# A k tile of the normed input 64 bytes off, and its two high products first in each chunk

## The chip, the cores and the metric

The kernel runs on one core of a Trainium2 chip. Its time is the device time of one execution in microseconds; the figure is the median of several executions. Of the engines, TensorE (PE in the profile; PEld is its loading of weights) multiplies matrices, VectorE (DVE) and ScalarE (ACT) work elementwise, GpSimd (POOL) does the rest, and SyncE (SP) issues the transfers of the weights.

## The reference, cut to what matters

Two layers work on 256 tokens of width 1024 in float32. Each layer norms its input, multiplies it with one wide matrix, feeds the parts to a sparse attention and to a state space scan, merges both with gates, projects, and adds a gated feed-forward block with a short convolution.

```python
for l in range(DEPTH):
    h = rms_norm(x, norm_mix_w[l])
    x = x + hybrid_mixer(h, w_in[l], ...)      # h @ w_in: q, k, v, index, z, xbc, dt, gates
    h = rms_norm(x, norm_ffn_w[l])
    x = x + conv_glu_ffn(h, ffn_w_up[l], ...)  # h @ w_up: 1024 x 5632; then w_down: 2816 x 1024
return rms_norm(x, norm_final_w)
```

In `conv_glu_ffn` the product `h @ w_up` goes through a causal convolution of width 3, one half through silu, and the product of both halves meets `w_down`.

## The kernel before, in words

A product in float32 is made of three products in a faster format: input and weights are each split into a high part and a low remainder, and high·high, high·low and low·high are added up in one accumulator. Weights come in chunks of 128 x 1024 numbers. SP loads a chunk into one of five `raw` buffers; ACT copies its high part (`whi`, line 199) and DVE subtracts it (`wlo`, line 200), into one of three pairs of buffers; a few chunks a layer are split early into tiles borrowed from activations (`ex`, `ez`, `es` and others in the trace). `take` (line 188) hands the next pair to the products and keeps loads and splits going. It then lets the side steps of the norm, the attention and the scan issue their instructions behind the last low product (`st["mm"]`), so that their products of other kinds come between those of the chunks.

`n_outer` (lines 390 to 397) computes 128 output columns for all 256 tokens: eight k tiles, each with a weight tile of 128 x 128, loaded into the array, and an input tile of 128 x 256 that moves through it. `feed_high` (line 367) issues whi·hi (line 370) and whi·lo (line 371) for each k, then `feed_low` (line 373) issues the eight wlo·hi (line 376): 24 products a chunk. `k_outer` does the same for four output tiles at once, over k, in a part of the projections.

The moving inputs are: the normed input `hxh`/`hxl`, [128, 8, 256] each, made by `Normed.scaled` (lines 341 to 349) and used by 92 `n_outer` chunks a layer (56 in the mix stage: convolution inputs, gates, z; 36 in the up projection); `uh`/`ul`, the input before the norm's factor; `aH`/`aL` (attention), `bH`/`bL` (scan), `mH`/`mL` (merged) and `fH`/`fL` (feed-forward), all split the same way. The last is cut over six pairs of tiles, the third and later ones of which lie in other tags than the first two. `row_of` (line 298) multiplies a matrix of ones with a diagonal `dg`, which is one of the foreign products in the stream.

A tile lies at one start address within each of the 128 partitions; pools and tags are laid out one behind the other, so a tag that grows moves all that lie after it. `mH`, the norm's `xw` and one early chunk share the tag of `hxh`. The small tile `dec` of the scan lies ahead of it.

Of the kernel before, what the change touches and what calls it, by code (L numbers as in the profile page):

```python
# [9 lines left out]
F32 = mybir.dt.float32  # L10
F32R = mybir.dt.float32r
# [7 lines left out]
P = 128  # L19
L = 2  # L20
T = 256
D = 1024
KD = D // P
# [8 lines left out]
TOPK = 64  # L32

RAW_BUFS = 5
SPLIT_BUFS = 3

FIRST_PAIRS = 4
# [25 lines left out]
def hybrid_kernel(ctx: ExitStack, tc: tile.TileContext, a: dict, out: bass.AP):  # L63
    nc = tc.nc

    const = ctx.enter_context(tc.tile_pool(name="const", bufs=1))
    wraw = ctx.enter_context(tc.tile_pool(name="wraw", bufs=RAW_BUFS))
    wsp = ctx.enter_context(tc.tile_pool(name="wsp", bufs=SPLIT_BUFS))
    act = ctx.enter_context(tc.tile_pool(name="act", bufs=1))
# [4 lines left out]
    def pst(tag, shape, bufs):  # L74
        t = psum.tile([P, 512], F32, name=tag, tag=tag, bufs=bufs)
        n = int(np.prod(shape[1:]))
        v = t[:shape[0], :n]
        if len(shape) == 3:
            v = v.rearrange("p (a b) -> p a b", a=shape[1])
        return v  # L80
# [88 lines left out]
    def load_some():  # L169
        while st["dma"] < len(order) and st["dma"] < st["prep"] + RAW_BUFS:  # L170
            i = order[st["dma"]]
            src, b, c = chunks[i]
            r = wraw.tile([P, 8 * 128], F32, name="raw", tag="raw")
            nc.sync.dma_start(r[:, :b * c].rearrange("p (b c) -> p b c", b=b), src)
            raws[i] = r[:, :b * c]
            st["dma"] += 1

    def split_tiles(j):
        if j in early:
            t0, t1 = early[j]  # L180
            if t0 == t1:
                t = act.tile([P, 2, 8 * 128], F32R, name=f"e{t0}", tag=t0)
                return [t[:, 0], t[:, 1]]
            return [(tmp if t in ("Xt", "pT") else act).tile([P, 8 * 128], F32R, name=f"e{t}", tag=t, bufs=1)
                    for t in (t0, t1)]
        return [wsp.tile([P, 8 * 128], F32R, name=t, tag=t) for t in ("whi", "wlo")]

    def take():
        i = st["cur"]
        with tc.high_priority():  # L190
            load_some()
            while st["prep"] < len(order):
                j = order[st["prep"]]
                if j not in early and sum(k not in early for k in splits) == SPLIT_BUFS:
                    break
                src, b, c = chunks[j]
                hi, lo = (t[:, :b * c] for t in split_tiles(j))
                r = raws.pop(j)
                nc.scalar.copy(out=hi, in_=r)  # L199
                nc.vector.tensor_sub(lo, r, hi.bitcast(F32))  # L200
                splits[j] = [t.rearrange("p (b c) -> p b c", b=b) for t in (hi, lo)]
                st["prep"] += 1
                load_some()
        st["cur"] += 1
        if st["mm"] is not None:
            side_steps()
        return splits.pop(i)
# [95 lines left out]
    class Normed:  # L303


        def __init__(self, nw, split=True):
            self.nw = nw
            self.acc = tmp.tile([P, T], F32, name="ssq", tag="ssq", bufs=3)
            if split:
                self.h = [act.tile([P, 4, T], F32R, name=f"uh{i}", tag=t) for i, t in enumerate(("Bm", "Cm"))]  # L310
                self.l = [act.tile([P, 4, T], F32R, name=f"ul{i}", tag=t) for i, t in enumerate(("lg0", "lg1"))]
            else:
                self.xw = act.tile([P, KD, T], F32, name="xw", tag="hxh")
            self.split = split

        def hi(self, k):
            return self.h[k // 4][:, k % 4, :]

        def lo(self, k):
            return self.l[k // 4][:, k % 4, :]  # L320
# [18 lines left out]
                nc.scalar.activation(self.xw[:, k, :], x, AF.Copy, scale=self.nw[:, k:k + 1])  # L339

        def scaled(self):
            h = act.tile([P, KD, T], F32R, name="hxh", tag="hxh")
            l = act.tile([P, KD, T], F32R, name="hxl", tag="hxl")
            for k in range(KD):
                t = tmp.tile([P, T], F32, name="ht", tag="ct", bufs=3)
                nc.vector.scalar_tensor_tensor(t, xT[:, k, :], self.nw[:, k:k + 1], self.row, op0=OP.mult, op1=OP.mult)
                nc.scalar.copy(out=h[:, k, :], in_=t)
                nc.vector.tensor_sub(l[:, k, :], t, h[:, k, :].bitcast(F32))
            return (lambda k: h[:, k, :]), (lambda k: l[:, k, :])

        def factor(self):
            ps = pst("sb", [P, 2], 2)
# [11 lines left out]
    def acc_tile():  # L364
        return pst("acc", [P, T], 4)

    def feed_high(ps, wh, hi, lo, ks, first):

        for j, k in enumerate(ks):
            nc.tensor.matmul(ps, wh[:, j, :], hi(k), start=first and j == 0, stop=False)  # L370
            nc.tensor.matmul(ps, wh[:, j, :], lo(k), start=False, stop=False)  # L371

    def feed_low(ps, wl, hi, ks, last):

        for j, k in enumerate(ks):
            st["mm"] = nc.tensor.matmul(ps, wl[:, j, :], hi(k), start=False, stop=last and j == len(ks) - 1)  # L376
# [13 lines left out]
    def n_outer(parts):  # L390

        ps = acc_tile()
        for i, (hi, lo, ks) in enumerate(parts):
            wh, wl = take()
            feed_high(ps, wh, hi, lo, ks, i == 0)
            feed_low(ps, wl, hi, ks, i == len(parts) - 1)
        return ps


# [5 lines left out]
    for l in range(L):  # L405
# [90 lines left out]
        dA = act.tile([P, 2, 32], F32, name="dA", tag="dA")  # L496
        Pc = act.tile([P, 2, 32], F32, name="Pc", tag="Pc")
        nP = act.tile([P, 2, 32], F32, name="nP", tag="nP")
        dec = act.tile([P, 32], F32, name="dec", tag="dec")

        prd = dram.tile([32, 2, P], F32, name=f"prd{l}")

# [36 lines left out]
        for c in range(5):  # L539
            n = 308 if c < 2 else 512  # L540
            pss = [pst("acc", [P, n], 4) for _ in range(2)]
            for j in range(4):
                wh, wl = take()
                for kk in range(2):
                    k = 2 * j + kk
# [28 lines left out]
        hi, lo = nrm.scaled()  # L574
# [69 lines left out]
        def conv_tile(i, dst):  # L644
            ps = n_outer([(hi, lo, range(KD))])
            v = tmp.tile([P, T], F32, name="cv", tag="cv", bufs=3)
            nc.scalar.activation(v, ps, AF.Identity, scale=cw(l, 3, i), bias=cb(l, i))  # L647
            for j in range(1, 4):
                nc.vector.scalar_tensor_tensor(v[:, j:], ps[:, :T - j], cw(l, 3 - j, i), v[:, j:],  # L649
                                               op0=OP.mult, op1=OP.add)  # L650
            th = tmp.tile([P, T], F32, name="ct", tag="ct", bufs=3)
            nc.scalar.activation(th, v, AF.Tanh)
            nc.vector.scalar_tensor_tensor(dst, th, 1.0, v, op0=OP.add, op1=OP.mult)

        def gate(t):
            ps = n_outer([(hi, lo, range(KD))])
            nc.scalar.activation(t, ps, AF.Tanh, scale=0.5)  # L657
            return t
# [101 lines left out]
        def gate_and_project(n):  # L760
            finish("attn")
            th = gate(tmp.tile([P, T], F32, name="gv", tag="cv", bufs=3))
            ps = n_outer([(lambda k: aH[k // 4][:, k % 4, :], lambda k: aL[k // 4][:, k % 4, :], range(8))])
            nc.vector.scalar_tensor_tensor(mg[n], th, 1.0, ps, op0=OP.add, op1=OP.mult)
# [24 lines left out]
        for g in range(4):  # L789
            finish("scan", 3 - g)  # L790
            y = xs[g]
            for i in range(4):
                ps = n_outer([(hi, lo, range(KD))])
# [14 lines left out]
            gate_and_project(n)  # L808


        mH = act.tile([P, KD, T], F32R, name="mH", tag="hxh")
        mL = act.tile([P, KD, T], F32R, name="mL", tag="hxl")
        bh = lambda k: bH[k // 4][:, k % 4, :]
        bl = lambda k: bL[k // 4][:, k % 4, :]
# [58 lines left out]
        hi, lo = nrm.scaled()  # L873
# [16 lines left out]
        for n in range(4, 8):  # L890
            ps = n_outer([(fh, fl, range(0, 8)), (fh, fl, range(8, 16)), (fh, fl, range(16, 22))])
# [6 lines left out]
    for c in range(2):  # L898
        for h in range(2):
            ps = pst("acc", [P, 512], 4)  # L900
# [93 lines left out]
```

## Time and profile before

| what | before |
|---|---|
| median of 3 runs | 1090.22 us (1088.49 to 1091.21) |
| the profiled execution | 1091.08 us, span 1089.1 us |
| TensorE busy | 1064.4 us, 98% |
| DVE, ACT, POOL busy | 81%, 64%, 6% |
| products of 128 x 256 with split weights | 7,416 |
| HBM | 175 GB/s over the span |

The span is the time from the first to the last recorded instruction. The profile models the end of a product, so its length (0.28 us) says little: products overlap, and what counts is the distance from one start to the next. In a timeline, neighbours of one line are drawn together with their count; the start of the next row then tells how long they took.

### The profile page before, as it was taken

How to read it: one execution, taken by the hardware profiler on the slowest of the kernel's cores; microseconds unless marked ns; L12 is line 12 of the kernel's file. 1: busy time of each engine (PE TensorE's matmuls, PEld its weight loads, DVE VectorE, ACT ScalarE, POOL GpSimd, SP SyncE). 2: the span in 40 equal slices, each digit the busy share in tenths (PEclk: the TensorE clock that was granted, in tenths of full speed). 3: DMA queues.
4: the chain of work that ended last, by engine and by line, in shares of the span. 5: the costliest groups of instructions: out<-in, count | busy, mean ns of one | idle time of the engine just before them, and what ended most of it. 6: DMA issues, size and time to landing. Idle time of an engine off the chain costs nothing.

```text
span 1089.1 us, 22471 instructions
## 1 busy us (share of the span) xinstructions
PE 1064.4 (98%) x8704; PEld 1026.2 (94%) x8704; DVE 877.9 (81%) x1755; ACT 696.2 (64%) x1285; POOL 66.5 (6%) x74
## 2 busy tenths in 40 slices
PE   6999999999999999998999999999999999999997
PEld 5789989999999999998997999999999999999997
DVE  6898988879877899885668999887887878888643
ACT  5658878647555576665555699865665556666552
POOL 3000000022000200000100000000310020000010
PEclk9999999999999999999999999999999999999999
DMA  7546444555677346666645654555567761666661
GB/s 266 183 148 213 151 147 156 161 169 175 194 233 251 117 122 195 194 199 211 183 134 176 224 155 139 164 172 155 175 190 216 246 216 45 182 187 191 180 182 48
DMA packets 52841, 191.82 MB, mean 176 GB/s; under 512 B 5952, under 2 KB 6240, under 8 KB 51712
## 3 DMA queue, kind: packets, MB, share of 16 engines
q1 hardware_dynamic: 50832, 180.31, 53.8%
q0 software_dynamic: 1472, 9.17, 2.3%
q8 instruction: 68, 1.11, 0.4%
q10 hardware_dynamic: 432, 0.92, 0.2%
q14 instruction: 37, 0.30, 0.1%
HBM read 189.26 MB, written 1.11 MB: 175 GB/s over the span
## 4 chain that ended last, share of the span: by engine, by line
PE 85%; DMA 5%; ACT 4%; DVE 3%; issue 2%; DVEq 0%; ACTq 0%; POOLq 0%
PE acc L370 23%; PE acc L371 23%; PE acc L376 23%; PE acc L550 3%; PE acc L551 2%; PE acc L549 2%; DMA bc<-prd 2%; DMA raw<-in_wu_dram 2%; PE sb L705 1%; DVE wlo L200 1%; ACT whi L199 1%; PE sa L461 1%; DVE ul L327 1%; PE sa L589 1%; PE sa L614 1%
## 5 line engine op out<-in xcount | busy, mean ns | idle before, releaser
L199 ACT CAST whi<-raw 128x1024 fp32r<-128x1024 f32 (+2 forms) x320 | 331.9, 1040 | 225.1 <-PE acc L371 168.7
L200 DVE TENSOR_TENSOR wlo<-raw,whi 128x1024 fp32r<-128x1024 f32 (+2 forms) x320 | 387.0, 1212 | 107.5 <-ACT whi L199 103.1
L370 PE MATMUL acc<-hxh,whi 128*128 128x256 f32 x1456 | 353.3, 282 | 1.0 <-ACT ths L657 0.9
L371 PE MATMUL acc<-hxl,whi 128*128 128x256 f32 x1456 | 351.2, 281 | 0.0
L370 PEld LDWEIGHTS acc<-hxh,whi 128*128 128x128 f32 x1456 | 274.6, 189 | 2.7 <-issue 1.1
L371 PEld LDWEIGHTS acc<-hxl,whi 128*128 128x128 f32 x1456 | 274.7, 189 | 2.2 <-issue 1.9
L376 PE MATMUL acc<-hxh,wlo 128*128 128x256 f32 x1456 | 202.2, 280 | 0.0
L376 PEld LDWEIGHTS acc<-hxh,wlo 128*128 128x128 f32 x1456 | 183.0, 189 | 0.7 <-issue 0.7
L370 PE MATMUL acc<-fH,whi 128*128 128x256 f32 x352 | 84.6, 280 | 2.8 <-DVE xT L833 2.8
L371 PE MATMUL acc<-fL,whi 128*128 128x256 f32 x352 | 84.4, 280 | 0.0
L649 DVE SCALAR_TENSOR_TENSOR cv<-acc,half,cv 128x255 f32<-128x255 f32 (+2 forms) x144 | 67.1, 474 | 3.9 <-ACT cv L647 3.4
L370 PEld LDWEIGHTS acc<-fH,whi 128*128 128x128 f32 x352 | 66.6, 190 | 3.1 <-issue 3.0
L851 DVE SCALAR_TENSOR_TENSOR cv<-acc,small,cv 128x255 f32<-128x255 f32 (+1 forms) x144 | 68.4, 477 | 1.3
L371 PEld LDWEIGHTS acc<-fL,whi 128*128 128x128 f32 x352 | 66.6, 189 | 0.0
L370 PE MATMUL acc<-bH,whi 128*128 128x256 f32 x256 | 62.4, 280 | 0.1
L371 PE MATMUL acc<-bL,whi 128*128 128x256 f32 x256 | 62.3, 282 | 0.0
L337 POOL TENSOR_TENSOR ssq<-ssq,sq 128x256 f32<-128x256 f32 x30 | 27.1, 904 | 516.8 <-ACT sq L333 516.2
L549 PE MATMUL acc<-whi,uh 128*128 128x512 f32 (+1 forms) x112 | 42.0, 392 | 9.2 <-ACT whi L199 9.2
L376 PE MATMUL acc<-fH,wlo 128*128 128x256 f32 x352 | 50.1, 281 | 0.0
L370 PEld LDWEIGHTS acc<-bH,whi 128*128 128x128 f32 x256 | 48.1, 188 | 0.4 <-issue 0.4
L371 PEld LDWEIGHTS acc<-bL,whi 128*128 128x128 f32 x256 | 48.2, 188 | 0.0
L695 ACT ACTIVATE bc<-bc,nP 128x128 f32<-128x128 f32 x128 | 39.9, 390 | 11.6 <-DMA bc<-prd 11.5
(281 smaller groups left out, 1873.0 us busy)
## 6 DMA issues: line engine op xcount, KB each, us to landing
raw<-in_wu_dram SPq DMA_DIRECT2D x88, 512.0 KB, 3.6
raw<-in_wx_dram SPq DMA_DIRECT2D x48, 512.0 KB, 3.6
raw<-in_wd_dram SPq DMA_DIRECT2D x38, 512.0 KB, 3.7
raw<-in_wz_dram SPq DMA_DIRECT2D x32, 512.0 KB, 3.6
raw<-in_wp_dram SPq DMA_DIRECT2D x32, 512.0 KB, 4.4
raw<-in_wq_dram SPq DMA_DIRECT2D x24, 512.0 KB, 4.5
raw<-in_wgs_dram SPq DMA_DIRECT2D x16, 512.0 KB, 3.6
bc<-prd POOLq DMA_DIRECT2D x8, 1024.0 KB, 7.3
```

The lines of the kernel that those rows point to most:

```text
L199: nc.scalar.copy(out=hi, in_=r)
L200: nc.vector.tensor_sub(lo, r, hi.bitcast(F32))
L337: nc.gpsimd.tensor_add(self.acc, self.acc, sq)
L370: nc.tensor.matmul(ps, wh[:, j, :], hi(k), start=first and j == 0, stop=False)
L371: nc.tensor.matmul(ps, wh[:, j, :], lo(k), start=False, stop=False)
L376: st["mm"] = nc.tensor.matmul(ps, wl[:, j, :], hi(k), start=False, stop=last and j == len(ks) - 1)
L549: nc.tensor.matmul(pss[t], nrm.hi(k)[:, s], wh[:, kk, :], start=f, stop=False)
L550: nc.tensor.matmul(pss[t], nrm.hi(k)[:, s], wl[:, kk, :], start=False, stop=False)
L551: st["mm"] = nc.tensor.matmul(pss[t], nrm.lo(k)[:, s], wh[:, kk, :], start=False, stop=e)
L649: nc.vector.scalar_tensor_tensor(v[:, j:], ps[:, :T - j], cw(l, 3 - j, i), v[:, j:], op0=OP.mult, op1=OP.add)
L695: nc.scalar.activation(E[:, h, :], E[:, h, :], AF.Relu, bias=nP[:, c, 8 * g + h:8 * g + h + 1])
L851: nc.vector.scalar_tensor_tensor(v[:, j:], uu[:, :T - j], fw(l, 2 - j, i), v[:, j:], op0=OP.mult, op1=OP.add)
```

## The change

The tile `hxh` gets 16 more numbers (64 B). Its k tile 0 stays at the start, the other seven lie 64 B further on. Other users of the tag leave the first 64 B out. `dec` is made 64 B longer, so that `hxh` itself starts 64 B later. In every part of an `n_outer` chunk the order of the first three products is high weights with high input, low weights with high input, high weights with low input, all for the first k tile; the pairs of the others follow, then the low weights of the others. The order applies to every user of `n_outer`, the 64 B to the normed input alone.

```diff
--- before.py
+++ after.py
@@ -32,6 +32,8 @@
 TOPK = 64
 
 RAW_BUFS = 5
+
+SHIFT = 16
 SPLIT_BUFS = 3
 
 FIRST_PAIRS = 4
@@ -175,9 +177,15 @@
             raws[i] = r[:, :b * c]
             st["dma"] += 1
 
+    def shifted(name, dtype):
+        return act.tile([P, SHIFT + KD * T], dtype, name=name, tag="hxh")[:, SHIFT:].rearrange("p (k t) -> p k t", k=KD)
+
     def split_tiles(j):
         if j in early:
             t0, t1 = early[j]
+            if t0 == "hxh":
+                t = shifted("ehxh", F32R).rearrange("p (a k) t -> p a (k t)", a=2)
+                return [t[:, 0], t[:, 1]]
             if t0 == t1:
                 t = act.tile([P, 2, 8 * 128], F32R, name=f"e{t0}", tag=t0)
                 return [t[:, 0], t[:, 1]]
@@ -310,7 +318,7 @@
                 self.h = [act.tile([P, 4, T], F32R, name=f"uh{i}", tag=t) for i, t in enumerate(("Bm", "Cm"))]
                 self.l = [act.tile([P, 4, T], F32R, name=f"ul{i}", tag=t) for i, t in enumerate(("lg0", "lg1"))]
             else:
-                self.xw = act.tile([P, KD, T], F32, name="xw", tag="hxh")
+                self.xw = shifted("xw", F32)
             self.split = split
 
         def hi(self, k):
@@ -339,14 +347,15 @@
                 nc.scalar.activation(self.xw[:, k, :], x, AF.Copy, scale=self.nw[:, k:k + 1])
 
         def scaled(self):
-            h = act.tile([P, KD, T], F32R, name="hxh", tag="hxh")
+            h = act.tile([P, SHIFT + KD * T], F32R, name="hxh", tag="hxh")
+            hs = [h[:, 0:T]] + [h[:, SHIFT + k * T:SHIFT + (k + 1) * T] for k in range(1, KD)]
             l = act.tile([P, KD, T], F32R, name="hxl", tag="hxl")
             for k in range(KD):
                 t = tmp.tile([P, T], F32, name="ht", tag="ct", bufs=3)
                 nc.vector.scalar_tensor_tensor(t, xT[:, k, :], self.nw[:, k:k + 1], self.row, op0=OP.mult, op1=OP.mult)
-                nc.scalar.copy(out=h[:, k, :], in_=t)
-                nc.vector.tensor_sub(l[:, k, :], t, h[:, k, :].bitcast(F32))
-            return (lambda k: h[:, k, :]), (lambda k: l[:, k, :])
+                nc.scalar.copy(out=hs[k], in_=t)
+                nc.vector.tensor_sub(l[:, k, :], t, hs[k].bitcast(F32))
+            return (lambda k: hs[k]), (lambda k: l[:, k, :])
 
         def factor(self):
             ps = pst("sb", [P, 2], 2)
@@ -392,8 +401,12 @@
         ps = acc_tile()
         for i, (hi, lo, ks) in enumerate(parts):
             wh, wl = take()
-            feed_high(ps, wh, hi, lo, ks, i == 0)
-            feed_low(ps, wl, hi, ks, i == len(parts) - 1)
+            k = ks[0]
+            nc.tensor.matmul(ps, wh[:, 0, :], hi(k), start=i == 0, stop=False)
+            nc.tensor.matmul(ps, wl[:, 0, :], hi(k), start=False, stop=False)
+            nc.tensor.matmul(ps, wh[:, 0, :], lo(k), start=False, stop=False)
+            feed_high(ps, wh[:, 1:], hi, lo, ks[1:], False)
+            feed_low(ps, wl[:, 1:], hi, ks[1:], i == len(parts) - 1)
         return ps
 
 
@@ -496,7 +509,7 @@
         dA = act.tile([P, 2, 32], F32, name="dA", tag="dA")
         Pc = act.tile([P, 2, 32], F32, name="Pc", tag="Pc")
         nP = act.tile([P, 2, 32], F32, name="nP", tag="nP")
-        dec = act.tile([P, 32], F32, name="dec", tag="dec")
+        dec = act.tile([P, 32 + SHIFT], F32, name="dec", tag="dec")[:, :32]
 
         prd = dram.tile([32, 2, P], F32, name=f"prd{l}")
 
@@ -808,7 +821,7 @@
             gate_and_project(n)
 
 
-        mH = act.tile([P, KD, T], F32R, name="mH", tag="hxh")
+        mH = shifted("mH", F32R)
         mL = act.tile([P, KD, T], F32R, name="mL", tag="hxl")
         bh = lambda k: bH[k // 4][:, k % 4, :]
         bl = lambda k: bL[k // 4][:, k % 4, :]
```

## Rows read from the trace of the kernel before

**Rows 1.** The page's first part: busy us, share of the span, instructions
```profile
PE 1064.4 (98%) x8704; PEld 1026.2 (94%) x8704; DVE 877.9 (81%) x1755; ACT 696.2 (64%) x1285; POOL 66.5 (6%) x74
```

**Rows 2.** The page's fourth part: the chain that ended last, by engine
```profile
PE 85%; DMA 5%; ACT 4%; DVE 3%; issue 2%; DVEq 0%; ACTq 0%; POOLq 0%
```

**Rows 3.** The page's fifth part: first group of weight products
```profile
L370 PE MATMUL acc<-hxh,whi 128*128 128x256 f32 x1456 | 353.3, 282 | 1.0 <-ACT ths L657 0.9
```

**Rows 4.** Windows: stretch, length, busy us (instructions) by engine, clock, DMA
```profile
385.97:483.90 97.93, 97.93 (x866) 97.93 (x865) 89.78 (x153) 67.89 (x113) 0.00 (x0) 1.00 0.62 185
483.91:549.09 65.18, 62.36 (x529) 62.19 (x528) 37.99 (x47) 31.50 (x46) 4.93 (x6) 0.97 0.66 197
915.56:1017.32 101.76, 101.76 (x866) 101.76 (x865) 89.56 (x153) 68.43 (x113) 0.00 (x0) 1.00 0.60 177
1017.32:1078.83 61.51, 61.51 (x530) 61.41 (x528) 28.54 (x32) 26.81 (x38) 5.07 (x6) 1.00 0.46 137
89.75:92.63 2.88, 2.88 (x26) 2.88 (x25) 0.81 (x1) 2.88 (x8) 0.00 (x0) 1.00 0.62 248
70.95:289.52 218.57, 217.26 (x1843) 208.01 (x1842) 190.11 (x406) 158.86 (x334) 17.43 (x16) 1.00 0.55 170
```

**Rows 5.** Timeline of TensorE: start, length, line, count; an early tile
```profile
91.56 0.28 PE L371 MATMUL acc<-hxl,ex 128*128 128x256 f32 x1
91.68 1.12 PE L376 MATMUL acc<-hxh,ex 128*128 128x256 f32 x8
92.63 0.28 PE L370 MATMUL acc<-hxh,whi 128*128 128x256 f32 x1
92.75 0.28 PE L371 MATMUL acc<-hxl,whi 128*128 128x256 f32 x1
```

**Rows 6.** Timeline of TensorE: `hxh` ends, `fH` begins, layer 0
```profile
483.23 0.84 PE L376 MATMUL acc<-hxh,wlo 128*128 128x256 f32 x6
483.91 0.28 PE L370 MATMUL acc<-fH,whi 128*128 128x256 f32 x1
484.03 0.28 PE L371 MATMUL acc<-fL,whi 128*128 128x256 f32 x1
```

**Rows 7.** Timeline of TensorE: from `fH`'s second tile to its third
```profile
494.27 1.10 PE L376 MATMUL acc<-fH,wlo 128*128 128x256 f32 x8
495.22 0.28 PE L370 MATMUL acc<-fH,whi 128*128 128x256 f32 x1
495.33 0.28 PE L371 MATMUL acc<-fL,whi 128*128 128x256 f32 x1
```

**Rows 8.** Timeline of TensorE: end of a `bH`/`bL` chunk
```profile
302.70 0.29 PE L371 MATMUL acc<-bL,whi 128*128 128x256 f32 x1
302.83 0.28 PE L370 MATMUL acc<-bH,whi 128*128 128x256 f32 x1
303.06 1.11 PE L376 MATMUL acc<-bH,wlo 128*128 128x256 f32 x8
304.01 0.28 PE L370 MATMUL acc<-bH,whi 128*128 128x256 f32 x1
```

**Rows 9.** Timeline of TensorE: the same with a row product
```profile
826.88 0.28 PE L298 MATMUL sb<-dg,ones 128*128 128x256 f32 x1
827.00 0.28 PE L371 MATMUL acc<-bL,whi 128*128 128x256 f32 x1
827.11 1.07 PE L376 MATMUL acc<-bH,wlo 128*128 128x256 f32 x8
828.02 0.28 PE L370 MATMUL acc<-bH,whi 128*128 128x256 f32 x1
```

**Rows 10.** Timelines of DVE and TensorE: a `wlo` tile, its first use
```profile
357.37 1.22 DVE L200 TENSOR_TENSOR wlo<-raw,whi 128x1024 fp32r<-128x1024 f32 x1
...
360.20 1.11 PE L376 MATMUL acc<-mH,wlo 128*128 128x256 f32 x8
```

**Rows 11.** Waits: engine, line, releaser: us in total, times, longest
```profile
ACT whi L199 <- PE acc L371: 168.7, 143, 5.4
```

## The prediction

> **What bounds the kernel now.** The page's busy shares come first: TensorE is busy for 98% of the span, at full granted clock [rows 1]. The chain that ended last runs through TensorE for 85% of the span, most of it the lines of the weight products [rows 2]. So the kernel ends when 7,416 products of 256 columns have been streamed, and the question is how far apart they start. `n_outer` with the normed input issues 184 chunks of 24 of them, 4,416 in all.
>
> Then the table of windows. The same 864 products of the up projection take 97.93 us in layer 0 and 101.76 us in layer 1 [rows 4], nothing else between them (the counts of 866 hold the two products that reach in from before): 113.3 and 117.8 ns from start to start. I call the two cadences F and S. Both hold for 36 chunks without a break, with the same code and data sizes, so a state lasts until something disturbs it. A third, E, is in the timeline where the weights lie in an early-split tile: 120 ns from start to start [rows 5], 24 products in 2.88 us [rows 4]. What sets E apart is addresses. In the compiled kernel before, `whi` and `wlo` start 64 B past a multiple of 512 in their partition, `hxh` and `hxl` at a multiple; the early tile `ex` starts at a multiple too, as `hxh` does. In E moving tile and weight tile have one position modulo 256 B. Otherwise the moving tile lies 64 B below the weights.
>
> All products at S instead of F would cost 4.44 ns each. Counting starts in the timeline, the excess over 113.3 ns (gaps of 130 ns and more left out) is 0.0 and 3.84 us in the two up projections, 3.94 and 3.96 us in the two mix stages (465 and 445 of 1,344 starts at F, 835 and 849 at S, layer 0's window holds 1,843 products in all [rows 4], layer 1's as many); 11.7 us in all. `fH` has 0.78 and 1.61 us (528 products in each of its windows [rows 4]), `aH` 0.67 us. That is what a change of this kind can give back.
>
> What moves the state? A jump of the moving address, or a foreign product. From `hxh` to `fH`, layer 0 goes from F to S within one product [rows 6]; at the fourth chunk boundary after, S goes to F [rows 7]. In `bH`/`bL` chunks every second product has its moving tile at the weights' position modulo 256 B (`bL`, as E) and the rest 64 B above it (`bH`). The eight `wlo` products that end such a chunk, all `bH`, then run at S: 0.95 us from first to next chunk [rows 8]. Of 32 such tails, 29 are S. Three are F, and two of these are the two where the row product `dg` (96 B off its weights) comes right ahead of the last `bL` product, so that two odd products follow each other: 0.91 us [rows 9].
>
> **The change, part by part.**
> *Addresses.* `dec` grows by 64 B and `hxh` starts after it: k tile 0 then lies 64 B past a multiple of 512, exactly where `whi` and `wlo` lie, which is the relation of E. The other k tiles, `hxl`, `mH`, `aH` and `fH` from its third tile on move by 128 B, to 64 B above the weights, the relation that `bH` and the first two tiles of `fH` have already. `bH`, `bL` and `uh` keep their places.
> *Order.* Each part of an `n_outer` chunk starts whi·hi0, wlo·hi0, whi·lo0; the rest is as before. Instructions, DMAs and bytes are the same in number, so nothing is added on ACT, DVE, POOL or SP. With `hxh`, each of 182 chunks (184 less the two with early tiles) starts with two products in E's relation.
> *The kick's own price.* Two products at 120 instead of 113.3 ns [rows 5, 4]: 13.3 ns from F, 4.4 ns from S. The exit was free behind E (92.63 to 92.75 us is 117 to 118 ns [rows 5]). I take 13.3 ns x 182 = 2.4 us; the ends are 0.8 us (all from S) and 5.5 us (30 ns: the longest interval behind a `bL` product is 0.13 us [rows 8], two of these are some 30 ns over two at F).
> *The state behind it.* This decides. 13.3 ns is three times 4.44, just the sum by which three S products fall behind F, so two E products put the stream off by one whole S period: from F the phase would be F's again. From S the nearest rows are the two pairs of odd products, and both ended in F, at the relation that `hxh` will have [rows 9]. I take F behind each kick. Against it stand the 29 tails behind a single one [rows 8], and both exits from E after 24 products, to S [rows 5].
> *What is left of S.* Foreign products fall into 21 and 27 of the 56 mix chunks per layer; behind the last one in a chunk 290 and 313 products remain. At S to the chunk's end they cost 603 x 4.44 ns = 2.7 us, at half that 1.3; I take 2.0 us.
> *`fH` and `aH`.* All of `fH` past its first two tiles now has the relation of these, so the jump between them [rows 7] goes. F lasts then if it enters in F. The bounds are -2.4 us (all F) and +2.2 us (all S: 4.6 for 2.4); I take -1.0. `aH`: -0.7 to +1.0, taken as 0.
> *`wlo` earlier.* It is wanted 15 products, 1.7 us, sooner. Between the end of `wlo`'s subtraction on DVE and its first product the median is 5.8 us, and the shortest in `n_outer` is in the `mH` chunk: DVE ends at 358.59 us, the first `wlo` product starts at 360.20 [rows 10]. With `wlo` wanted at 358.4 that chunk waits 0.2 us; the same in layer 1: +0.4 us. Behind a waiting product stands all of TensorE. If the cover were gone everywhere each chunk would wait for DVE; with 5.8 us I put that at nothing.
> *`whi` one product longer.* ACT waits 168.7 us in all for `whi` buffers, 143 times [rows 11]; their release comes 0.12 us later each time. TensorE's first products with `hxh` sat idle for 1.0 us in all, behind ACT's `ths` and not behind `whi` [rows 3], so this costs nothing; were ACT the bound, 0.12 us a chunk.
>
> Sum for the likeliest case: `hxh` 2.4 + 2.0 - 11.7 = -7.3, `fH` -1.0, `wlo` +0.4: -7.9 us on the profiled 1091.1, so 1083.2. The median of the runs shown is 0.9 below that execution, which makes 1082.3; I say 1082.5.
>
> [...]
>
> **The rivals.**
> *A, the kick locks the slow state.* Every `hxh` chunk then runs at S. For it: 29 of 32 tails behind an odd product at the very relation that `hxh` gets [rows 8], both exits from E [rows 5], and F to S at the jump to `fH`'s first tiles, which have that relation too [rows 6]. Against it: the two pairs [rows 9]. Price: 4,416 x 4.44 ns less the starts behind gaps, 19.2 us, for 11.7 now: +7.5; kicks from S +0.8; `aH` up to +1.0, `fH` up to +2.2; +0.4 for `wlo`. +8.7 to +11.9, 1099 to 1102. It beats the gain as soon as over 60% of the products stay at S, which is today's share (11.7 of 19.2).
> *C, no lasting lock.* The state behind a kick depends on the phase in which it comes, and each chunk draws anew; or it hangs on something else than the address. Half at S: 9.6 us + kicks of 8.9 ns x 182 = 1.6, 11.2 for 11.7 now; with `fH` and `aH` to either side 1088 to 1093, 1090 in the middle. For it: the foreign products of the mix stage change the state in about half the cases and not in the others. [...]
> *D, `wlo` comes late.* If DVE's lead shrinks because TensorE runs faster, waits of the size of that in [rows 10] spread. Tens of them cost 4 us; DVE is busy for 81% [rows 1], against.
>
> **How the numbers follow.** Likeliest, F behind each kick: 0.50, own range 1079 (kick cheap, all of `fH` F) to 1087 (kick 5.5, 2.7 left, `fH` no better). A: 0.26, C: 0.22, D: 0.02. The range 1079 to 1099 leaves out half of A, D, and a little below. 0.3% is 3.3 us, about what a measurement of this kernel can tell from no change. Faster by more: 0.47 + 0.03 of C. Within: 0.03 of the likeliest, 0.15 of C. Slower: A, D and the rest of C, 0.32.
>
> **What would show it.** After the change, the windows of the two up projections should both last some 98.4 us (864 x 113.3 ns + 36 kicks of 13.3 ns); the first two intervals of each chunk 240 ns together; in the mix stages each chunk's first products at F whatever came before. If each is some 102 us, A holds; if the layers or the chunks differ, C. I am wrong if F is entered by only some kicks, if the kick costs more than 30 ns, or if products wait at the second slot of a chunk.

## The result, and the profile after

The changed kernel takes 1097.11 us in the median of 5 runs (1095.77 to 1097.99), the kernel before 1088.49 in as many. The ratio is 1.0084, with a 95% interval of 1.0060 to 1.0108: slower, by rival A's mechanism.

First the changed kernel's page, the first and fourth part and two groups of the fifth (line, tiles, count, busy us and mean ns of one, idle time before).

```profile
PE 1071.8 (98%) x8704; PEld 1033.4 (94%) x8704; DVE 877.7 (80%) x1755; ACT 695.6 (64%) x1285; POOL 65.7 (6%) x74
...
PE 91%; DMA 3%; DVE 3%; issue 1%; ACT 1%; DVEq 0%; ACTq 0%; POOLq 0%
...
L379 PE MATMUL acc<-hxh,whi 128*128 128x256 f32 x1274 | 311.2, 280 | 0.0
...
L405 PE MATMUL acc<-hxh,whi 128*128 128x256 f32 x182 | 53.4, 294 | 0.1
```

TensorE is as full as before [rows 1] and its part of the chain has grown from 85% to 91% [rows 2]: the products themselves got longer in sum, 1071.8 us busy for 1064.4, with the same 8,704 of them. Next the table of windows (stretch, length, busy us and count by engine, clock, DMA): layer 0's mix stage, its up projection, the down projection, and layer 1's up projection.

```profile
70.85:289.29 218.44, 218.34 (x1843) 209.65 (x1842) 189.72 (x406) 159.08 (x334) 16.92 (x16) 1.00 0.54 170
386.41:488.18 101.77, 101.77 (x867) 101.77 (x865) 89.50 (x154) 67.69 (x114) 0.00 (x0) 1.00 0.60 178
488.18:550.39 62.21, 62.21 (x530) 62.13 (x528) 38.40 (x47) 31.86 (x46) 5.12 (x6) 1.00 0.67 207
919.64:1021.41 101.77, 101.77 (x866) 101.77 (x865) 89.18 (x153) 66.92 (x113) 0.00 (x0) 1.00 0.59 177
```

Against [rows 4]: the up projection of layer 0 has gone from 97.93 to 101.77 us, layer 1's stays at 101.77, both now 117.8 ns a product. Counting from start to start, the weight products' excess over 113.3 ns (gaps of 130 ns and more apart) rises by 9.3 us: up projections +3.8, mix stages from 3.94 and 3.96 to 5.43 and 5.62 (+3.2), `fH` from 0.78 and 1.61 to 2.34 each (+2.3: not one product of 1,056 at 113.3 ns), `aH` +0.7, `uh` -0.6. Gaps of 130 ns and more fell by 3.1 us; stalls of 4.7 us in layer 0's down projection, which the changed kernel's execution does not have, are more than that: 65.18 us there [rows 4], 62.21 here. Products of other kinds took 1.3 us less. So the two profiled spans stand 4.9 us apart, the medians 8.6.

The timeline of TensorE at the first chunk of layer 0's up projection shows one kick from cadence F:

```profile
386.41 0.28 PE L405 MATMUL acc<-hxh,whi 128*128 128x256 f32 x1
386.53 0.28 PE L406 MATMUL acc<-hxh,wlo 128*128 128x256 f32 x1
386.65 0.28 PE L407 MATMUL acc<-hxl,whi 128*128 128x256 f32 x1
386.77 0.28 PE L379 MATMUL acc<-hxh,whi 128*128 128x256 f32 x1
386.89 0.28 PE L380 MATMUL acc<-hxl,whi 128*128 128x256 f32 x1
```

The two equal-position products (lines 405 and 406) and the one behind them take 0.12 us each, 119, 120 and 122 ns by the unrounded starts, and the stream goes on at 117.8 ns. Of the kicks with a plain cadence on both sides (four intervals before, the five behind the first three products), all 11 that came in F ended in S, and all 125 that came in S stayed there. Of the 20 right behind a foreign product five ended in F (at 112.3, 119.5, 135.2, 633.1 and 639.6 us), until the next kick. A chunk in S takes 2,827 ns, exactly 24 x 117.8: from S the kick costs nothing, and does nothing.

The wait for `wlo` that was priced at 0.4 us is there once, for 0.2 us (waits of TensorE: us in total, times, longest):

```profile
PE acc L406 <- DVE wlo L208: 0.2, 1, 0.2
```

Between the starts at 358.96 and 359.36 us lies no other, also none of the products behind that need no `wlo` (line 407 and on).

### The profile page after: what moved, and what is told of

Same layout as the page of the kernel before. It is cut to its first block, busy times and chain, and to the rows that moved or that the text cites. A ratio compares the mean times of both kernels' runs of the same rounds, so it can differ in the third digit from the quotient of the medians.

```text
span 1094.0 us, 22476 instructions
## 1 busy us (share of the span) xinstructions
PE 1071.8 (98%) x8704; PEld 1033.4 (94%) x8704; DVE 877.7 (80%) x1755; ACT 695.6 (64%) x1285; POOL 65.7 (6%) x74
## 4 chain that ended last, share of the span: by engine, by line
PE 91%; DMA 3%; DVE 3%; issue 1%; ACT 1%; DVEq 0%; ACTq 0%; POOLq 0%
PE acc L380 22%; PE acc L379 22%; PE acc L385 22%; PE acc L563 3%; PE acc L564 3%; PE acc L405 3%; PE acc L562 3%; PE acc L407 3%; PE acc L406 3%; DMA raw<-in_wu_dram 2%; PE sb L718 2%; DVE wlo L208 1%; PE sa L602 1%; DVE ul L335 1%; PE sa L474 1%
## 5 line engine op out<-in xcount | busy, mean ns | idle before, releaser
L380 PE MATMUL acc<-hxl,whi 128*128 128x256 f32 x1274 | 312.1, 281 | 0.0
L379 PE MATMUL acc<-hxh,whi 128*128 128x256 f32 x1274 | 311.2, 280 | 0.0
L380 PEld LDWEIGHTS acc<-hxl,whi 128*128 128x128 f32 x1274 | 239.0, 188 | 0.6 <-issue 0.5
L379 PEld LDWEIGHTS acc<-hxh,whi 128*128 128x128 f32 x1274 | 239.3, 188 | 0.3 <-issue 0.2
L385 PE MATMUL acc<-hxh,wlo 128*128 128x256 f32 x1274 | 182.5, 280 | 0.0
L385 PEld LDWEIGHTS acc<-hxh,wlo 128*128 128x128 f32 x1274 | 163.4, 188 | 0.6 <-issue 0.5
L379 PE MATMUL acc<-fH,whi 128*128 128x256 f32 x328 | 79.6, 279 | 0.0
L380 PE MATMUL acc<-fL,whi 128*128 128x256 f32 x328 | 79.6, 279 | 0.0
L379 PEld LDWEIGHTS acc<-fH,whi 128*128 128x128 f32 x328 | 61.5, 188 | 0.0
L380 PEld LDWEIGHTS acc<-fL,whi 128*128 128x128 f32 x328 | 61.5, 188 | 0.0
L405 PE MATMUL acc<-hxh,whi 128*128 128x256 f32 x182 | 53.4, 294 | 0.1
L407 PE MATMUL acc<-hxl,whi 128*128 128x256 f32 x182 | 51.1, 281 | 0.0
L406 PE MATMUL acc<-hxh,wlo 128*128 128x256 f32 x182 | 50.9, 280 | 0.0
```

The source lines that it names most:

```text
L405: nc.tensor.matmul(ps, wh[:, 0, :], hi(k), start=i == 0, stop=False)
L406: nc.tensor.matmul(ps, wl[:, 0, :], hi(k), start=False, stop=False)
L407: nc.tensor.matmul(ps, wh[:, 0, :], lo(k), start=False, stop=False)
```

## The experiments

Theory 1: a moving tile 64 B above its weights runs at 117.8 ns by itself. Theory 2: the products at the weights' own position (the kick) put the stream there. Theory 3: the order does it. As the prediction does, the texts call a k tile's place the same as the weights', or 64 B above or below it, modulo 256 B.

**The order alone.** The kernel before with the changed order of the first three products, all tiles where they were.

```diff
-            feed_high(ps, wh, hi, lo, ks, i == 0)
-            feed_low(ps, wl, hi, ks, i == len(parts) - 1)
+            k = ks[0]
+            nc.tensor.matmul(ps, wh[:, 0, :], hi(k), start=i == 0, stop=False)
+            nc.tensor.matmul(ps, wl[:, 0, :], hi(k), start=False, stop=False)
...
```

> The new order of the first three products alone; every tile lies where it lay before. Theory 1 (the place of the moving tile 64 B above its weights holds the stream at 117.8 ns) and theory 2 (the two products at the weights' own position set it back to 117.8 ns) both expect the time of the kernel before, 1083 to 1091 us, with a cadence of 113.3 or 117.8 ns in each up projection by chance. A theory 3, that the order does it, expects 1095 to 1098 us and 117.8 ns in both up projections.

1086.52 us against 1089.06, ratio 0.9981 (0.9963 to 0.9999). The windows of its two up projections:

```profile
386.02:487.79 101.77, 101.77 (x867) 101.77 (x865) 89.88 (x154) 67.64 (x114) 0.00 (x0) 1.00 0.60 179
916.93:1014.86 97.93, 97.93 (x866) 97.93 (x865) 88.93 (x152) 66.81 (x112) 0.00 (x0) 1.00 0.61 184
```

One at S and one at F, the other way round than before [rows 4]. The order costs nothing: theory 3 falls.

Which of the two cadences an up projection gets is not chance in these traces. The last products ahead of it have `uh` as their input and the early tile `epT` as their weights; in the kernel before, layer 0 and then layer 1:

```profile
385.16 0.98 PE L376 MATMUL acc<-uh,epT 128*128 128x256 f32 x7
385.98 0.28 PE L370 MATMUL acc<-hxh,whi 128*128 128x256 f32 x1
...
915.00 0.73 PE L376 MATMUL acc<-uh,epT 128*128 128x256 f32 x5
915.57 0.28 PE L370 MATMUL acc<-hxh,whi 128*128 128x256 f32 x1
```

Seven products in 0.82 us are S, and the up projection behind them runs at F; five in 0.57 us are F, and S follows. So it is in all six up projections that begin without a kick, 64 B below the weights (the kernel before, this one, and the first probe further down): four times S became F, twice F became S. With the input 64 B above, F stayed F, four times of four (the next kernel and the second probe).

**All of the input 64 B above, no tile apart.** The old order; `dec` grows by 128 B.

```diff
-        dec = act.tile([P, 32], F32, name="dec", tag="dec")
+        dec = act.tile([P, 32 + 32], F32, name="dec", tag="dec")[:, :32]
```

> The old order and an unbroken normed input, all of it (and all that lies after it) moved up by 128 B to 64 B above the weights; no k tile lies apart. Theory 1 expects the changed kernel's time, 1095 to 1098 us, with 117.8 ns in both up projections and in the down projections. Theory 2 expects what the kernel before has, 1083 to 1091 us, with stretches at 113.3 ns.

1088.24 us, ratio 0.9993 (0.9974 to 1.0011). Its up projections:

```profile
386.57:484.50 97.93, 97.93 (x867) 97.93 (x866) 89.92 (x154) 68.02 (x114) 0.00 (x0) 1.00 0.61 186
918.04:1015.96 97.92, 97.92 (x866) 97.92 (x865) 89.50 (x153) 67.36 (x113) 0.00 (x0) 1.00 0.62 184
```

Both at F, 864 products in a row in each, at the relation that the changed kernel's other tiles have to the weights. Theory 1 falls for the up projections: the place above the weights permits both cadences. In the mix stages it holds in part: the excess there is 5.3 and 5.2 us, for 3.9 and 4.0 before and 5.4 and 5.6 in the changed kernel. There, among foreign products, the place alone brings most of the rise (5.3 us in each layer of the second probe too); in this execution the two up projections at F make up for it.

**The offset tile with the old order.** The changed kernel's addresses, `n_outer` as before: two single products at the weights' position, 16 places apart, for the pair.

```diff
-            k = ks[0]
-            nc.tensor.matmul(ps, wh[:, 0, :], hi(k), start=i == 0, stop=False)
...
+            feed_high(ps, wh, hi, lo, ks, i == 0)
+            feed_low(ps, wl, hi, ks, i == len(parts) - 1)
```

> The changed kernel's addresses with the old order: the high product of k tile 0 comes first, its low-weight product 16 places later, so that two single products at the weights' position take the place of the pair. If only a pair sets the slow cadence, single ones leave either cadence and the time is that of the kernel before, 1084 to 1091 us. If any product at the weights' position does it above the weights, 1095 to 1098 us, both up projections at 101.8 us.

1097.15 us, ratio 1.0088 (1.0067 to 1.0108), the whole of the loss. Up projections:

```profile
387.07:488.61 101.54, 101.54 (x866) 101.54 (x865) 90.03 (x153) 68.73 (x113) 0.00 (x0) 1.00 0.59 180
923.33:1024.86 101.53, 101.53 (x866) 101.53 (x865) 89.55 (x153) 68.25 (x113) 0.00 (x0) 1.00 0.58 178
```

117.5 ns a product in both: S, but for one interval of 113 ns in each chunk. No pair is needed; with the rest of the input above the weights, a product at their position is enough. These three undo the change part by part: order alone and move alone leave the time, the k tile apart brings the whole loss. By the starts, against the kernel with the move alone, it brings 7.2 us in the up projections, 2.3 us in `fH` and 0.6 us in the mix stages.

**The pair, with the rest below the weights.** The new order and k tile 0 at the weights' position, but the others where they were before the change. (Two small tiles, `rot` and `pr`, which share two buffers, get one, which pays for the 256 B.)

```diff
+            h = act.tile([P, KD * T + 64], F32R, name="hxh", tag="hxh")
+            hs = [h[:, 7 * T + 16:8 * T + 16]] + [h[:, (k - 1) * T:k * T] for k in range(1, KD)]
...
```

> The new order and k tile 0 at the weights' own position, but all other tiles where they lay before, 64 B below the weights (k tile 0 moved behind the others, 256 B more for the tile, paid for by one buffer less of two small ones). Theory 2 expects the changed kernel's 1095 to 1098 us, both up projections at 117.8 ns. Theory 1 expects that 113.3 ns is to be had again: each up projection 98 to 102 us, 36 chunks with up to 13 ns each for the two products, the time 1081 to 1092 us.

1089.29 us, ratio 0.9994 (0.9978 to 1.0009). Three chunks in a row, then the two up projections:

```profile
387.86:390.69 2.83, 2.83 (x27) 2.83 (x26) 2.79 (x6) 2.77 (x6) 0.00 (x0) 1.00 0.00 0
390.69:393.43 2.74, 2.74 (x26) 2.74 (x25) 2.74 (x6) 1.48 (x3) 0.00 (x0) 1.00 0.67 196
393.43:396.25 2.82, 2.82 (x26) 2.82 (x25) 2.50 (x6) 2.26 (x5) 0.00 (x0) 1.00 0.83 199
385.11:485.32 100.21, 100.21 (x867) 100.21 (x865) 89.62 (x154) 67.63 (x114) 0.00 (x0) 1.00 0.61 182
915.18:1015.39 100.21, 100.21 (x866) 100.21 (x865) 89.00 (x152) 66.91 (x112) 0.00 (x0) 1.00 0.60 180
```

2.83, 2.74, 2.82: the pair turns F into S and S into F, chunk by chunk, in 71 of the 72; layer 0's first, behind `uh`'s products at F, ended in F. Half the chunks gain and half lose, so the time stands still. What a kick does within the normed input is a rule and not a draw, and the rule depends on the side on which the rest lies: in the changed kernel, above the weights, the same pair ended in S from F as from S. Theory 2 holds for the changed kernel and is incomplete.

**How many products, on which side.** A probe for the rule: in the up projections copies of the first k tiles lie at the weights' position, and a chunk begins with n products from there. All else is 64 B below the weights, as in the kernel before, or 64 B above (`dec` grows by 128 B).

```diff
+KICKS = ([0, 0, 1, 1, 1, 0, 2, 2, 2, 0, 3, 3, 3, 0, 4, 4, 4, 0, 5, 5, 5, 0, 1, 2, 1, 2, 1, 0, ...]
...
+                for j, (w, high, k) in enumerate(seq[:kick]):
+                    nc.tensor.matmul(ps, w[:, k, :], away(high, k), start=j == 0, stop=False)
...
+        copies = act.tile([P, 8, T], F32R, name="copies", tag="big0")
...
```

> Addresses as in the kernel before (64 B below the weights). In the up projections the first k tiles are copied once more to the weights' own position, and a chunk begins with n products from there: n is 1, 2, 3, 4, 5 in three chunks each with a plain chunk behind in layer 0, 6 to 10 and 12 in layer 1. The combined theory (the pair of equal-position products sets the cadence, and to which one depends on the side on which the rest lies) expects n = 2 to change 113.3 to 117.8 ns and back, as it did chunk by chunk in the kick below the weights, and each n to have a fixed rule of its own; plain chunks keep what they are given. The theory that chance alone sets the cadence expects no rule: equal n with unequal outcomes from the same cadence.

Below (1089.97 us in its one run): six chunks of layer 0 with n = 1, 2, 2, 3, 3 and 5.

```profile
395.50:398.25 2.75, 2.75 (x27) 2.75 (x25) 2.75 (x7) 1.89 (x4) 0.00 (x0) 1.00 0.60 192
403.71:406.54 2.83, 2.83 (x27) 2.83 (x26) 2.79 (x7) 1.74 (x4) 0.00 (x0) 1.00 0.66 197
406.54:409.28 2.74, 2.74 (x26) 2.74 (x25) 2.54 (x5) 1.78 (x4) 0.00 (x0) 1.00 0.57 187
414.93:417.68 2.75, 2.75 (x26) 2.75 (x25) 2.48 (x5) 1.98 (x5) 0.00 (x0) 1.00 0.62 191
417.68:420.42 2.74, 2.74 (x26) 2.74 (x25) 2.63 (x6) 1.81 (x4) 0.00 (x0) 1.00 0.53 185
437.12:439.88 2.76, 2.76 (x26) 2.76 (x25) 2.28 (x4) 1.61 (x4) 0.00 (x0) 1.00 0.76 208
```

A chunk with a kick that ends in F takes 2.74 to 2.80 us, one that ends in S 2.82; read from its last products, the rule is the same each time:

| n | from F | from S |
|---|---|---|
| 1 | F (5 of 5) | S (1 of 1) |
| 2 | S (5 of 5) | F (3 of 3) |
| 3 | F (2 of 2) | F (2 of 2) |
| 4 | S (2 of 2) | F (1 of 1) |
| 5 | F (2 of 2) | F (1 of 1) |
| 6 to 10, 12 | F (16 of 16) | not met |

Plain chunks kept what they were given. Chance falls, and three products in a row are a kick that ends in F from either cadence, at 2,740 ns a chunk from F (20 ns over 2,720).

> The same probe with the rest 64 B above the weights, as in the changed kernel without its offset k tile. The combined theory expects 117.8 ns behind every n = 2, from either cadence, and that a stretch at 113.3 ns can still come from another n or stand before the first. The theory of chance expects both cadences behind n = 2.

Above: a plain chunk, then n = 1, 2, 3 and 4.

```profile
388.85:391.57 2.72, 2.72 (x27) 2.72 (x26) 2.40 (x5) 2.72 (x5) 0.00 (x0) 1.00 0.00 0
391.57:394.40 2.83, 2.83 (x27) 2.83 (x26) 2.83 (x7) 2.53 (x5) 0.00 (x0) 1.00 0.64 191
402.88:405.71 2.83, 2.83 (x26) 2.83 (x25) 2.69 (x6) 1.69 (x4) 0.00 (x0) 1.00 0.60 194
414.19:417.02 2.83, 2.83 (x27) 2.83 (x26) 2.54 (x5) 2.02 (x5) 0.00 (x0) 1.00 0.68 194
425.52:428.27 2.75, 2.75 (x26) 2.75 (x25) 2.27 (x4) 1.72 (x4) 0.00 (x0) 1.00 0.64 188
```

The first kick, one product at 391.57 us, turned F into S, and of 40 kicks of all sizes one (n = 4, at 425.52) led back to F, until the next kick. Every other ended in S: 8 of 8 with n = 2, 4 of 4 with n = 3. But 37 of the 40 came in S already. From F came only n = 1, 4 and 6, once each, so for n = 2 from F the changed kernel's 11 kicks have to stand. The program took 1098.13 us in its one run.

**128 B off.** Old order; input and all behind it 128 B off the weights.

```diff
-        dec = act.tile([P, 32], F32, name="dec", tag="dec")
+        dec = act.tile([P, 32 + 48], F32, name="dec", tag="dec")[:, :32]
```

> The old order, the normed input and all behind it moved up by 192 B, to 128 B above the weights (modulo 256 B as far below). If positions count modulo 128 B, this is the relation of the early tiles: 120 ns throughout, 4,416 products x 6.7 ns = 29 us for the 11.7 above 113.3 ns that the kernel before has, with the attention's and down projection's products 1105 to 1112 us. If they count modulo 256 B, the relation is a new one: by theory 1 each relation has its own set of cadences, so between 113.3 ns throughout (1079 us) and 117.8 ns throughout (1097 us).

1105.31 us, ratio 1.0147 (1.0124 to 1.0170).

```profile
388.62:492.30 103.68, 103.68 (x866) 103.68 (x865) 90.03 (x153) 69.54 (x113) 0.00 (x0) 1.00 0.59 177
928.00:1030.52 102.52, 102.52 (x866) 102.52 (x865) 89.43 (x152) 68.47 (x112) 0.00 (x0) 1.00 0.59 176
```

Layer 0's up projection runs at 120.0 ns a product, as with an early tile [rows 5]; layer 1's at 118.7, in a pattern of five products of 115 to 122 ns. By the cadence, 128 B off is nearly the same as 0 off, and the time lies at the lower end of what positions modulo 128 B forecast. That 64 B above and 64 B below still differ says that modulo 128 is not all either.

**A version built on the rule.** Rest below the weights, and the low input's k tile 0 at the weights' position too, so that the changed order starts each chunk with three such products.

```diff
+            l = act.tile([P, KD * T + 64], F32R, name="hxl", tag="hxl")
+            ls = [l[:, 7 * T + 16:8 * T + 16]] + [l[:, (k - 1) * T:k * T] for k in range(1, KD)]
...
```

> The changed kernel's order with three products in a row at the weights' own position (k tile 0 of the high and of the low input), all else 64 B below the weights. The probe there found 113.3 ns behind three products from either cadence, at 2,740 ns a chunk from 113.3 and 2,752 from 117.8. If that is a rule: both up projections 98.6 us (36 x 2.740), the normed input's 184 chunks 3.7 us above 113.3 ns and some 1.5 to 2.5 us behind foreign products in the mix stages, where the kernel before has 11.7: 1081 to 1085 us, under before. If it was chance: one up projection or both near 101 us, 1086 to 1092.

1082.33 us (1080.63 to 1085.27), ratio 0.9952 (0.9936 to 0.9968).

```profile
383.23:481.98 98.75, 98.75 (x866) 98.75 (x865) 89.39 (x153) 67.52 (x113) 0.00 (x0) 1.00 0.61 184
909.12:1007.78 98.66, 98.66 (x867) 98.66 (x865) 89.07 (x153) 66.92 (x113) 0.00 (x0) 1.00 0.62 182
```

98.75 and 98.66 us, as forecast; 2.740 us for 69 of 72 chunks. The first of layer 0 came behind `uh`'s products at S and stayed at S (2,843 ns), the second set F.

**Three products once.** The version above, with plain copies of k tile 0, 64 B below the weights, for all but the first chunk of each up projection.

```diff
+        near = act.tile([P, 48 + 2 * T], F32R, name="near", tag="big1")
...
+        hj, lj = (lambda k: hi(k) if k else near[0]), (lambda k: lo(k) if k else near[1])
...
+            pg = n_outer([(hi, lo, range(8))] if i == 4 else [(hj, lj, range(8))])
+            pv = n_outer([(hj, lj, range(8))])
```

> The same, but in each up projection only the first chunk begins with the three products; the other 35 take a copy of k tile 0 that lies 64 B below the weights. If the cadence lasts until something disturbs it, both up projections stay at 113.3 ns, 97.95 us each, and the time is 1.4 us under the kernel with three products in each chunk: 1080 to 1084 us. If the three products have to come again in each chunk, the up projections fall back to 117.8 ns, 101.8 us.

1085.54 us (1080.26 to 1088.42), ratio 0.9979 (0.9961 to 0.9998).

```profile
383.87:485.64 101.77, 101.77 (x866) 101.77 (x865) 89.62 (x153) 67.65 (x113) 0.00 (x0) 1.00 0.60 180
913.25:1011.21 97.96, 97.96 (x866) 97.96 (x865) 89.08 (x154) 67.05 (x112) 0.00 (x0) 1.00 0.63 184
```

Layer 1 did as hoped; in layer 0 the one kick, behind `uh` at S, failed again and S stayed for 36 chunks, so the time missed its 1080 to 1084 us. Both show that a cadence lasts.

**Three products twice.** In the first two chunks, against the version above.

```diff
-            pv = n_outer([(hj, lj, range(8))])
+            pv = n_outer([(hi, lo, range(8))] if i == 4 else [(hj, lj, range(8))])
```

> As the kernel with three products in the first chunk of each up projection, but in its first two chunks. There layer 0's first chunk of 2,843 ns took over 117.8 ns and kept it for 36 chunks; in the kernel with three products in each chunk the same first chunk was followed by one of 2,752 ns at 113.3. If the rule of the three products holds from an undisturbed cadence, the second chunk sets 113.3 ns in both layers, 34 plain chunks keep it, and the time is 1079.5 to 1083.5 us, under the kernel with three in each chunk (1082.3). If plain chunks fall out of 113.3 ns by themselves, 1083 to 1088.

1080.27 us (1078.43 to 1082.95), ratio 0.9923 (0.9897 to 0.9948): faster than the kernel before.

```profile
382.62:480.60 97.98, 97.98 (x866) 97.98 (x865) 89.55 (x155) 67.91 (x113) 0.00 (x0) 1.00 0.61 186
908.53:1006.60 98.07, 98.07 (x866) 98.07 (x865) 88.84 (x152) 67.12 (x112) 0.00 (x0) 1.00 0.63 183
```

Layer 1's first kick behind `uh` failed this time (2,843 ns), the second set F (2,752), and 34 plain chunks of 2,720 follow, in both layers. Over the three versions the kick of three behind `uh` failed all three times that `uh`'s products ran at S, and kept F all three times that they ran at F.

**Three products above the weights.** The changed kernel with the low input's k tile 0 apart as well.

```diff
+            l = act.tile([P, KD * T + 64], F32R, name="hxl", tag="hxl")
+            ls = [l[:, 7 * T + 48:8 * T + 48]] + [l[:, (k - 1) * T:k * T] for k in range(1, KD)]
...
```

> The changed kernel with the low input's k tile 0 at the weights' own position as well, so that three products in a row lie there, and all else 64 B above the weights. If the number of products alone decides, three set 113.3 ns here too and the up projections take 98.6 us. If the side decides with it, as in the probe above the weights (117.8 ns behind three, four times of four), they take 101.7 to 102.1 us and the time is 1095 to 1099 us.

1099.21 us in one run.

```profile
388.11:490.59 102.48, 102.48 (x867) 102.48 (x866) 89.72 (x153) 67.67 (x113) 0.00 (x0) 1.00 0.59 179
922.34:1024.81 102.47, 102.47 (x866) 102.47 (x865) 89.25 (x153) 67.03 (x113) 0.00 (x0) 1.00 0.59 176
```

102.48 and 102.47 us, S with 20 ns more a chunk. Layer 1's first kick came behind products at F (as did one in a mix stage, at 710.9 us) and ended in S; the others of the up projections came in S and stayed. What sets F below the weights sets S above: the side decides.

## Why the prediction was wrong

*That the cadence of the products bounds the kernel, and that the edit acts on it alone.* Right. The starts' +9.3 us stand beside 8.6 us between the medians, and taken apart, the change moved the time only where it moved the cadence. The full clock stands in [rows 4], not in [rows 1], and the 7,416 products hold the 24 of `row_of`; 7,392 have split weights.

*The state behind it: "I take F behind each kick".* This step failed. The argument from phase (two products at 120 ns put the stream off by 13.3 ns, one whole S period, so from F back to F) is refuted on both sides of the weights: F goes to S behind a pair, 11 of 11 above, and below 5 of 5 in the probe and 36 of 36 in the toggling kernel, its first chunk behind `uh` apart. The two pairs of [rows 9] that ended in F held a product of `dg`, 96 B off its weights, and a single `bL`. They were not a pair at the weights' own position, and were let outweigh 29 tails [rows 8] whose other products lay 64 B above the weights, as the changed kernel's do. Those 29, given to rival A, were the rule: of the probe's kicks above the weights only one in 40 led elsewhere.

*The size that followed.* `hxh`, forecast at -7.3 us, rose from 11.7 to 18.7, +7.0, close to rival A's +7.5 (19.2 in all). Of that, the mix stages' +3.2 needed a term that the sum lacks: the move from below to above the weights, which brought 2.7 us there without any kick. `fH`, taken at -1.0, came to +2.3, A's bound: the jump did go, as foretold, but `fH` entered in S behind `hxh` and kept it; `aH`, taken at 0, to +0.7. The kick's price of 2.4 us is nothing, since from S the pair takes two S intervals. `wlo`, +0.4, came to 0.2. A's sum of +8.7 to +11.9 stands beside +9.3 in the starts, and 1099 to 1102 beside 1097.1. That 1097.1 lies inside 1079 to 1099 speaks for no step of the likeliest case: that end of the range was drawn for A.

*The relation modulo 256 B.* Half wrong: 128 B off gave 120 ns in layer 0 and 118.7 in layer 1.

*"What sets E apart is addresses."* The runs bear out that addresses count. Between the kernel with all input 64 B above the weights and the one with it 128 B above lies nothing but 64 B of padding, and 864 products took 97.93 and 97.92 us in the one (101.77 at S elsewhere), 103.68 and 102.52 us in the other. What in the chip makes addresses count was not measured.

*Left open.* Why the side matters, why `uh`'s cadence decides what follows it, what sets `uh`'s own, and how many phases S has: above the weights chunks with n = 3, all from S, took 2,824 to 2,846 ns.

## What to carry to other kernels

When one loop's products run at two cadences with equal code, look for a state that lasts, and find the rule that sets it with a probe that varies one cause over the chunks of a single run, before building on it. An event that resembles the change from afar (two odd products of another kind) weighs less than many that share its exact relation. A kernel whose time depends on such a state may spread from run to run: timed side by side, before took 1084.9 to 1092.0 us in 11 runs, the version with the state set twice 1078.4 to 1083.0 in 6. That the cadence makes this spread is likely but not shown: one execution of each kernel was traced.

## What the runs showed of the hardware

Products of 256 columns with their weights' loading started every 113.3, 117.8 or 120 ns at full granted clock (1.00 in the windows of the up projections), by the start addresses of moving tile and weight tile and by what came before (118.7 on average in one up projection, 128 B off). A cadence lasted for 860 products and more. With the input 64 B below the weights, n products in a row at the weights' position toggled the cadence for n = 2 and 4, left it for n = 1, and set 113.3 ns for n = 3 and 5; with the input 64 B above, 39 of the probe's 40 kicks ended at 117.8 ns, 37 of which had come at it. Where the moving input changed from `uh` to an unkicked `hxh` 64 B below the weights, 113.3 and 117.8 ns changed places, six times of six. A product of 256 columns in float32 itself (line 589 of the kernel before) has two records in the trace, with starts 215 ns apart.
